# A squared-ReLU MLP by seven block products: the down stage run product by product, sums of its weights kept in DRAM, the up results stored without splitting

## The chip, the cores and the metric

The kernel runs on 1 core of one Trainium2 chip. A core has a matrix engine (TensorE, PE in the rows), a vector engine (DVE), a scalar engine (ACT), GpSimd (POOL) and a sync engine (SP), which run their own instruction streams in order and wait for each other by semaphores. PE writes its sums into eight PSUM banks; all other data lies in SBUF tiles of 128 partitions or in DRAM, and moves between the two by DMA. The metric is the device time of one execution in microseconds (us); lower is better.

## The reference, cut to what matters

```python
def sq_relu_mlp(h, w1, w2):
    return jnp.square(jax.nn.relu(h @ w1)) @ w2
...
        x = x_mid + gt_f * sq_relu_mlp(modulate(rms_norm(x_mid, g_ffn[l]), sh_f, sc_f),
                                       w_ff1[l], w_ff2[l])
    return rms_norm(x, g_final)
```

h is 1024 x 1024, w1 1024 x 4096, w2 4096 x 1024, all in 32-bit floats. Ahead of this stand a modulated norm, an input projection, retention heads, latent attention and the output projection; they make x_mid and are not touched.

## The kernel before

**Numbers.** A product of two 32-bit matrices is made from three matmuls: each operand is split into a rounded half (hi, type fp32r, written by ACT with a cast) and the rest (lo, a subtraction on DVE); hi·hi, hi·lo and lo·hi are summed in PSUM (`split`, lines 102 to 104, `mm3`, lines 97 to 100).

**Seven products.** Both matrix products of the MLP are done on 2 x 2 blocks with seven block products (numbered q = 1 to 7) instead of eight. Their operands are blocks or sums of blocks, and the seven results are added into the four result blocks: products 1, 6 and 7 one after the other into one PSUM sum ("a"), 5 and 3 into another ("c"), 2 and 4 into one each.

**Up stage.** Loop over 16 pairs p of 128 + 128 hidden columns. For each (p, q), `prep1` splits a piece of w1 (casts at L103, subtractions at L104), `mm_1` issues 12 matmuls of 128x512, and `post1` empties the bank: the copy at L1177 takes the sum of (p,6) out before (p,7) may add to the same bank, L1179 does so after (p,7), L1162 after (p,2). Relu and square are L1143 and L1144. With the last product, (p,3), the four hidden blocks c11, c12, c21, c22 are there; four subtractions and additions on DVE make the operands s1 to s4 of the down stage. c11 is stored in DRAM as `uda`, c21 and c22 as `udy`, s1 and s2 as `udz`, s3 and s4 as `udw`. `store_u` splits y, z and w before storing (cast L1152, subtraction through the helper at L94) and stores both halves (L1154, L1155), 1 MB for each instead of 512 KB.

**Down stage.** The contraction is cut into NB = 4 blocks b of GB = 4 pairs. The outer loop runs over b, the inner over the products q = 2, 1, 6, 5, 3, 7, 4. A step (b, q) has 4 row tiles k of 12 matmuls; after each, the bank is added to the result tiles `acc` in SBUF (a copy at L1271 the first time). `load_u` fetches the stored halves over POOL's DMA queue (L1237; `uda` over SP), `load_w2` the four blocks of w2 over SP (L1211), `chain_w2` and `chain2_w2` make the sums T1 to T4 of w2 blocks with `pairop` (L1085), and `prep2` splits the w2 operand. For the last block w2 is multiplied by the gate beforehand (`gate_w2`). The residual x_mid (`xm`) is added by `to_mid` along the way, and `final` normalizes and writes a row tile.

**Order.** All work is issued from Python loops in program order; a scheduler then orders each engine's stream by its own estimates. SBUF comes from a pool of 45 slots of 512 KB (`sl.get`, `sl.put`): a freed slot goes to the end of a queue and the next request takes the first. An instruction that gets a slot waits for the last user of it, which may be a DMA that still stores from it. In the up stage, `order` is the list of the (p, q), and `prep1` runs LEAD + 1 = 5 entries ahead; e = -1 is its last entry. In the last 11 entries the first loads and splits of the down stage are mixed in.

Of the kernel before, what the change touches and what calls it, by code (L numbers as in the profile page):

```python
# [12 lines left out]
F32 = mybir.dt.float32  # L13
# [40 lines left out]
def hymba_block(ctx: ExitStack, tc: tile.TileContext, A, K, out):  # L54
# [987 lines left out]
    while pend:  # L1042
# [115 lines left out]
    def post1(p, q):  # L1158
# [13 lines left out]
        if q == 1:  # L1172
            tt(c11, ps, c11, ALU.add)
            sqrelu(c11)
            store_u("a", p, x_, x_[0][:, 0:1])
        elif q == 6:
            S.copy(out=c12, in_=ps)  # L1177
        elif q == 7:
            S.copy(out=c21, in_=ps)  # L1179
            unbank(p, q)  # L1180
            tt(c22, bank(p, 5), c21, ALU.add)
        elif q == 4:
            tt(c21, c21, ps, ALU.subtract)
            unbank(p, q)
            sqrelu(c21)
            sqrelu(c22)
        elif q == 3:
            tt(c12, ps, c12, ALU.add)
            unbank(p, q)
            sqrelu(c12)  # L1190
            z, w = sl.get((2, 512)), sl.get((2, 512))
            s1, s2, s3, s4 = z[0][:, 0], z[0][:, 1], w[0][:, 0], w[0][:, 1]
            tt(s1, c12, c22, ALU.add)
            tt(s2, s1, c11, ALU.subtract)
            tt(s3, c11, c12, ALU.subtract)
            tt(s4, c21, s2, ALU.subtract)
            store_u("y", p, y_, y_[0])
            store_u("z", p, z, z[0])
            store_u("w", p, w, w[0])
            sl.put(x_)  # L1200
            cq.pop(p)

    w2r, w2v = {}, w_ff2.rearrange("(g i p) c -> i p g c", i=2, p=P)

    def load_w2(b, qs=("B21", "B11", "B12", "B22")):
        for q in qs:
            i, j = BH[q]
            w2r[b, q] = [sl.get((2, 512)) for _ in range(GB // 2)]
            for v, r in enumerate(w2r[b, q]):
                g = b * GB + 2 * v  # L1210
                nc.sync.dma_start(out=r[0], in_=w2v[i, :, g:g + 2, j * 512:(j + 1) * 512])  # L1211

    def chain_w2(b):
        n = GB // 2
        r = lambda q: w2r[b, q]
        for q in ("T1", "T2"):
            w2r[b, q] = [sl.get((2, 512)) for _ in range(n)]
        pairop(V, r("T1"), r("B12"), r("B11"), ALU.subtract)
        pairop(V, r("T2"), r("B22"), r("T1"), ALU.subtract)
        pairop(V, r("B12"), r("B22"), r("B12"), ALU.subtract)  # L1220
        w2r[b, "T3"] = w2r.pop((b, "B12"))

    def chain2_w2(b):
        pairop(V, w2r[b, "B21"], w2r[b, "B21"], w2r[b, "T2"], ALU.subtract)
        w2r[b, "T4"] = w2r.pop((b, "B21"))
        sl.put(*w2r.pop((b, "T2")))

    UOF = {1: ("a", 0), 2: ("y", 0), 4: ("y", 1), 5: ("z", 0), 6: ("z", 1), 7: ("w", 0), 3: ("w", 1)}
    ur, ab = {}, {}

    def load_u(b, q):
        n, k = UOF[q]
        vs = (0,) if n == "a" else (0, 1)
        ur[b, q] = [[sl.get((2, 512), F32 if n == "a" else F32R) for _ in range(GB // 2)] for _ in vs]
        for x_ in vs:
            for v, r in enumerate(ur[b, q][x_]):
                (nc.sync if n == "a" else nc.gpsimd).dma_start(out=r[0], in_=ud[n, b, x_][:, k, 2 * v:2 * v + 2, :])  # L1237

    def prep2(b, q):
        u_, w_ = ur.pop((b, q)), w2r[b, BOF[q]]  # L1240
        new = lambda: [[sl.get((2, 512), F32R) for _ in range(GB // 2)] for _ in range(2)]
        if len(u_) == 1:
            raw, u_ = u_[0], new()
            for v in range(GB // 2):
                split(raw[v][0], u_[0][v][0], u_[1][v][0])
            sl.put(*raw)
        ab[b, q] = [u_, new()]
        for v in range(GB // 2):
            split(w_[v][0], ab[b, q][1][0][v][0], ab[b, q][1][1][v][0])
        if q not in (2, 6):  # L1250
# [4 lines left out]
    def mm_2(b, q, k):
        (ah, al), (bh, bl) = ab[b, q]
        key = (b, k, {1: "a", 6: "a", 7: "a", 2: "b", 5: "c", 3: "c", 4: "d"}[q])
        if key not in pb:
            pb[key] = pF()
        ps = pb[key]  # L1260
        w = slice(k * P, (k + 1) * P)
        for g in range(GB):
            v, i = g // 2, g % 2
            mm3(ps, ah[v][0][:, i, w], al[v][0][:, i, w], bh[v][0][:, i], bl[v][0][:, i],
                q in (1, 2, 4, 5) and g == 0, g == GB - 1, q in (3, 6, 7))
        lo_, hi_ = slice(0, 512), slice(512, 1024)
        t0, t1 = acc[k][0], acc[4 + k][0]
        for o, first in {1: [(t0[:, lo_], False)], 2: [(t0[:, lo_], True)], 6: [(t0[:, hi_], True)], 5: [(t1[:, hi_], True)],
                         3: [(t0[:, hi_], False)], 7: [(t1[:, lo_], True), (t1[:, hi_], False)], 4: [(t1[:, lo_], False)]}[q]:
            if first and b == 0:  # L1270
                S.copy(out=o, in_=ps)  # L1271
            else:
                tt(o, ps, o, ALU.add)
# [7 lines left out]
    def load_xm(t):  # L1281
        xr_[t] = sl.get((1024,))
        nc.sync.dma_start(out=xr_[t][0], in_=xm[t])

    fs = {}

    def final(t):
# [3 lines left out]
        n = 2 if t == NT - 1 else 1  # L1291
# [77 lines left out]
    steps2 = [(b, q) for b in range(NB) for q in (2, 1, 6, 5, 3, 7, 4)]  # L1369
    for s, (p, q) in enumerate(order):  # L1370
# [3 lines left out]
        print("S", s - len(order), s, p, q, len(sl.free), file=open("/tmp/sl.txt", "a"))  # L1374
# [31 lines left out]
    for t in range(NT):
        acc[t] = sl.get((1024,))
    HALF = slice(0, 512), slice(512, 1024)

    def gate_w2(b, q, v):  # L1410
        r = w2r[b, q][v]
        tt(r[0], r[0], bc[5][0][:, HALF[BH[q][1]]].unsqueeze(1).broadcast_to([P, 2, 512]), ALU.mult)

    def load_xm(t, h):
        xr_[t, h] = tmp()
        nc.sync.dma_start(out=xr_[t, h], in_=xm[t][:, HALF[h]])

    def to_mid(t, h):
        w = acc[t][0][:, HALF[h]]
        tt(w, w, bc[5][0][:, HALF[h]], ALU.mult)  # L1420
        tt(w, w, xr_.pop((t, h)), ALU.add)

    s0 = 7 * (NB - 2)
    mids = [[(k, 0) for k in range(4)], [(k, 1) for k in range(4)], [(4 + k, 1) for k in range(4)], [(4 + k, 0) for k in range(4)]]
    side = {}
    for g, a in zip(mids, (s0 + 2, s0 + 6, s0 + 8, s0 + 10)):
        for n, m in enumerate(g):
            side.setdefault((a + n // 2, 1 + n % 2 * 2), []).append(lambda m=m: to_mid(*m))
            side.setdefault((a + n // 2 - 1, n % 2 * 2), []).append(lambda m=m: load_xm(*m))
    for n, (q, v) in enumerate([(q, v) for q in ("B21", "B11", "B12", "B22") for v in range(GB // 2)]):  # L1430
        side.setdefault((s0 + 4 + n // 4, n % 4), []).append(lambda q=q, v=v: gate_w2(NB - 1, q, v))

    def squares(t, h):
        if t not in fs:
            fs[t] = small.tile([P, 2], F32, name=f"fs{t}", tag=f"fs{t}", bufs=1)
        S.activation(out=tmp(), in_=acc[t][0][:, HALF[h]], func=AF.Square, accum_out=fs[t][:, h:h + 1])

    for s, (b, q) in enumerate(steps2):
        last = b == NB - 1
# [70 lines left out]
```

## Time and profile before

| | |
|---|---|
| median of 3 runs | 1331.37 us (1330.32 to 1335.32) |
| profiled execution | 1329.17 us, span 1327.4 us |
| PE busy | 1275.3 us, 96% of the span, 6665 matmuls |
| DVE busy | 973.9 us (73%) |
| ACT busy | 644.5 us (49%) |
| SP's DMA queue (q1) | 156.56 MB |
| POOL's DMA queue (q0) | 58.49 MB |
| mean granted PE clock | 0.988 of full |

The up stage's products with stores run from about 692 us, the down stage from about 1000 us to 1318 us. The tail behind it is the last normalization and its store. "Busy" for PE is modelled: a matmul is shown 0.39 us long although the next starts 0.227 us later, so idle time stands out only in the rows on waits and in counts of matmuls per stretch.

### The profile page before, as it was taken

To read this page: it belongs to the slowest core of one execution; us is meant where nothing else is said; L and a number is where in the kernel's file an instruction comes from. 1 tells how busy PE (TensorE), PEld (TensorE's weight loads), DVE (VectorE), ACT (ScalarE), POOL (GpSimd) and SP (SyncE) were. 2 spreads that over 40 slices of the span, in tenths; PEclk is the share of its full clock that TensorE was granted. 3 is DMA by queue.
4 is the path that set the end of the run, shared out by engine and by line. 5 is a ranking of instruction groups with operands and counts; after the bars stand their busy time and mean duration, and the time that the engine had idled before them with its cause. 6 is when DMAs were issued, how large, how long until landed. Compare 5 with 4: busy or idle time off the path is not lost.

```text
span 1327.4 us, 18159 instructions
## 1 busy us (share of the span) xinstructions
PE 1275.3 (96%) x6665; PEld 1086.9 (82%) x6665; DVE 973.9 (73%) x1950; ACT 644.5 (49%) x1349; POOL 73.4 (6%) x133
## 2 busy tenths in 40 slices
PE   7899999999999999999999799999987999999997
PEld 7788888999999898878788578887866788887885
DVE  5898576664777767984796788878767374876976
ACT  1851256754556545732475576766654231221233
POOL 0100000000000000000000000000001111111110
PEclk9999999999999999999999899999989999999999
DMA  9508401300001004362521577765799958577753
GB/s 348 213 3 290 153 28 53 100 13 0 1 9 36 9 25 143 104 214 96 162 84 51 211 276 247 270 225 205 245 338 341 373 159 289 202 257 259 215 158 125
DMA packets 98667, 216.73 MB, mean 163 GB/s; under 512 B 9353, under 2 KB 29522, under 8 KB 98578
## 3 DMA queue, kind: packets, MB, share of 16 engines
q1 hardware_dynamic: 81634, 156.56, 34.0%
q0 software_dynamic: 16368, 58.49, 13.3%
q8 instruction: 52, 0.85, 0.3%
q10 hardware_dynamic: 576, 0.53, 0.1%
q14 instruction: 37, 0.30, 0.1%
HBM read 148.70 MB, written 66.85 MB: 162 GB/s over the span
## 4 chain that ended last, share of the span: by engine, by line
PE 51%; issue 30%; DMA 8%; DVE 6%; ACT 4%; POOL 1%; SPq 0%; DVEq 0%; ACTq 0%; POOLq 0%
PE ps L100 15%; PE ps L98 15%; PE ps L99 15%; DMA u<-in_w_ff_dram 3%; DVE u L94 2%; PE ps L280 2%; DMA udw<-u 1%; DVE u L104 1%; ACT u L1152 1%; PE ps L238 1%; DMA udy<-u 1%; DMA u<-udy 1%; ACT u L103 1%; DVE u L502 1%; DMA u<-k_tri_dram 1%
## 5 line engine op out<-in xcount | busy, mean ns | idle before, releaser
L98 PE MATMUL ps<-u,u 128*128 128x512 f32 (+3 forms) x1664 | 621.5, 375 | 27.8 <-ACT u L103 8.0
L100 PE MATMUL ps<-u,u 128*128 128x512 f32 (+3 forms) x1664 | 613.3, 370 | 2.6 <-DVE u L94 1.7
L99 PE MATMUL ps<-u,u 128*128 128x512 f32 (+3 forms) x1664 | 614.8, 370 | 0.0
L98 PEld LDWEIGHTS ps<-u,u 128*128 128x128 f32 x1664 | 315.4, 190 | 86.0 <-ACT u L103 10.4
L100 PEld LDWEIGHTS ps<-u,u 128*128 128x128 f32 x1664 | 314.7, 189 | 54.8 <-DVE u L104 2.3
L99 PEld LDWEIGHTS ps<-u,u 128*128 128x128 f32 x1664 | 315.3, 189 | 49.0 <-issue 0.5
L103 ACT CAST u<-u 128x1024 fp32r<-128x1024 f32 (+3 forms) x199 | 168.1, 862 | 228.5 <-PE ps L99 66.5
L94 DVE TENSOR_TENSOR u<-ps,u 128x512 f32<-128x512 f32 (+3 forms) x318 | 201.7, 648 | 87.0 <-PE ps L100 62.0
L104 DVE TENSOR_TENSOR u<-u,u 128x1024 fp32r<-128x1024 f32 (+4 forms) x197 | 189.2, 982 | 59.6 <-ACT u L103 50.1
L94 DVE TENSOR_TENSOR u<-u,u 128x512 f32<-128x512 f32 (+2 forms) x128 | 114.9, 919 | 35.2 <-DMA u<-in_w_ff_dram 15.1
L863 DVE TENSOR_REDUCE mx<-ps 128x1 f32<-128x512 f32 (+1 forms) x96 | 55.0, 594 | 25.8 <-PE ps L862 25.7
L1152 ACT CAST u<-u 128x1024 fp32r<-128x1024 f32 x48 | 49.3, 1049 | 35.6 <-DVE u L94 29.8
L897 ACT CAST u<-ps 128x512 fp32r<-128x512 f32 (+1 forms) x96 | 45.1, 530 | 21.2 <-PE ps L895 21.2
L1085 DVE TENSOR_TENSOR u<-u,u 128x1024 f32<-128x1024 f32 x40 | 47.7, 1216 | 3.4 <-DMA u<-in_w_ff_dram 3.3
L1143 ACT ACTIVATE u<-u 128x512 f32<-128x512 f32 x64 | 40.1, 627 | 20.2 <-DVE u L94 19.9
L874 ACT ACTIVATE u<-ps,nm 128x512 f32<-128x512 f32 x64 | 43.6, 691 | 11.8 <-DVE nm L867 11.8
L1144 ACT ACTIVATE u<-u 128x512 f32<-128x512 f32 x64 | 40.3, 631 | 1.1
L427 DVE SCALAR_TENSOR_TENSOR u<-u,sc,u 128x1024 f32<-128x1024 f32 x28 | 35.8, 1279 | 4.5 <-DMA u<-in_w_ada_dram 4.2
L1237 POOL DMA_DIRECT2D u<-udy x32 | 16.9, 534 | 371.7 <-DVE u L104 314.9
L858 PE MATMUL ps<-u,u 128*128 128x512 f32 (+1 forms) x96 | 37.1, 387 | 0.4 <-ACT u L837 0.2
L280 PE MATMUL ps<-u,u 128*128 128x128 f32 x224 | 29.1, 295 | 8.6 <-DMA u<-in_w_ada_dram 8.6
L104 DVE TENSOR_TENSOR u<-tmp,u 128x512 fp32r<-128x512 f32 x32 | 21.8, 687 | 19.3 <-ACT u L103 19.3
(209 smaller groups left out, 1290.1 us busy)
## 6 DMA issues: line engine op xcount, KB each, us to landing
u<-in_w_ff_dram SPq DMA_DIRECT2D x64, 512.0 KB, 7.0
u<-in_w_ada_dram SPq DMA_DIRECT2D x48, 512.0 KB, 5.5
udy<-u SPq DMA_DIRECT2D x32, 512.0 KB, 3.6
udz<-u SPq DMA_DIRECT2D x32, 512.0 KB, 3.8
udw<-u SPq DMA_DIRECT2D x32, 512.0 KB, 5.3
u<-udy POOLq DMA_DIRECT2D x32, 512.0 KB, 7.0
u<-udz POOLq DMA_DIRECT2D x32, 512.0 KB, 6.6
u<-udw POOLq DMA_DIRECT2D x32, 512.0 KB, 7.7
```

What stands on the lines that cost most here:

```text
L94: V.tensor_tensor(out=o, in0=a, in1=b, op=op)
L98: T.matmul(ps, lhsT=lh, rhs=rh, start=start, stop=False, **kw)
L99: T.matmul(ps, lhsT=lh, rhs=rl, start=False, stop=False, **kw)
L100: T.matmul(ps, lhsT=ll, rhs=rh, start=False, stop=stop, **kw)
L103: S.copy(out=hi, in_=raw)
L104: (eng or V).tensor_tensor(out=lo, in0=raw, in1=f(hi), op=ALU.subtract)
L280: T.matmul(mps[g][j // 4][:, j % 4, :], lhsT=w[:, j * P:(j + 1) * P], rhs=rhs, start=first and j % 4 == 0, stop=last and j % 4 == 3)
L863: V.reduce_max(out=mx[:, kb:kb + 1], in_=ps[:, 0:n], axis=AX.X)
L874: S.activation(out=dst[kb], in_=ps[:, 0:n], func=AF.Exp, scale=SCALE, bias=nm, accum_out=su[:, kb:kb + 1])
L897: S.copy(out=hi, in_=ps[:, 0:m, :])
L1085: eng.tensor_tensor(out=o[v][0], in0=a[v][0], in1=b[v][0], op=op)
L1152: S.copy(out=h[0], in_=ap)
```

## The change

- `store_u` stores y, z and w as they are: its casts, subtractions and second DMAs are gone. Each slot goes back to the pool after the stores. The splitting is done in the down stage, in `prep2`.
- GB becomes 2, so the contraction has NB = 8 blocks, and the outer loop of the down stage is the product: steps (q, b) for q = 2, 1, 6, 7, 4, 5, 3, each with all eight b. A PSUM bank keeps its sum over the eight steps; it is emptied after the last b alone (`evac2`). A step has 4 row tiles of 6 matmuls. In the last four steps of product 3 the row tile is the outer loop.
- A step loads its u operand (512 KB) and one or two w2 tiles (512 KB each), all over SP's queue. Product 1's steps make T1 = B12 - B11 and store it in DRAM (`td`), product 6's make T2 = B22 - T1 likewise; later steps load them back. Loads are issued up to six steps ahead, splits up to three.
- The gate is no longer folded into w2: `to_mid` multiplies result halves by it, and `evac2` does for product 3.

```diff
-    NP, GB = FF // 256, 4
+    NP, GB = FF // 256, 2
...
-    def store_u(q, p, r, ap):
-        if q == "a":
-            nc.sync.dma_start(out=ud[q, p // GB, 0][:, :, p % GB, :], in_=ap)
-            return
-        h = sl.get((2, 512), F32R)
-        lo = ap.bitcast(F32R)
-        S.copy(out=h[0], in_=ap)
-        tt(lo, ap, f(h[0]), ALU.subtract)
-        nc.sync.dma_start(out=ud[q, p // GB, 0][:, :, p % GB, :], in_=f(h[0]))
-        nc.sync.dma_start(out=ud[q, p // GB, 1][:, :, p % GB, :], in_=f(lo))
-        sl.put(h, r)
+    def store_u(q, p, ap):
+        nc.sync.dma_start(out=ud[q, p // GB][:, :, p % GB, :], in_=ap)
...
+    WOF = {2: ("B21",), 1: ("B11", "B12"), 6: ("B22", "T1"), 7: ("B22", "B12"), 4: ("B21", "T2"), 5: ("T1",), 3: ("B22",)}
+    steps2 = [(q, b) for q in (2, 1, 6, 7, 4, 5, 3) for b in range(NB)]
...
+    def load2(s):
+        q, b = steps2[s]
         n, k = UOF[q]
...
+        raw2[s] = r = [sl.get((2, 512)) for _ in range(1 + len(WOF[q]))]
+        nc.sync.dma_start(out=r[0][0], in_=ud[n, b][:, k])
+        for w, t in zip(WOF[q], r[1:]):
+            if w in BH:
+                i, j = BH[w]
+                nc.sync.dma_start(out=t[0], in_=w2v[i, :, b * GB:(b + 1) * GB, j * 512:(j + 1) * 512])
+            else:
+                nc.sync.dma_start(out=t[0], in_=td[w, b])
+
+    def prep2(s):
+        q, b = steps2[s]
+        u, w, *x_ = raw2.pop(s)
+        ab[s] = [sl.get((2, 512), F32R) for _ in range(4)]
+        split(u[0], ab[s][0][0], ab[s][1][0])
+        sl.put(u)
+        if q in (6, 7, 4):
+            tt(w[0], w[0], x_[0][0], ALU.subtract)
+        split(w[0], ab[s][2][0], ab[s][3][0])
+        if q == 1:
+            tt(x_[0][0], x_[0][0], w[0], ALU.subtract)
+            nc.sync.dma_start(out=td["T1", b], in_=x_[0][0])
         if q == 6:
...
+            nc.sync.dma_start(out=td["T2", b], in_=w[0])
+        sl.put(*x_, w)
...
+        else:
+            m = tmp()
+            tt(m, ps, bc[5][0][:, hi_], ALU.mult)
+            tt(t0[:, hi_], m, t0[:, hi_], ALU.add)
+            squares(k, 1)
+            final(k)
...
+        e = s - len(order)
+        if e in (-10, -8, -6, -4):
+            load2((10 + e) // 2)
+        if e in (-5, -3):
+            prep2((5 + e) // 2)
...
+        while nload < min(s + 7, len(steps2)):
+            load2(nload)
+            nload += 1
+        while nprep < min(s + 4, len(steps2)):
+            prep2(nprep)
+            nprep += 1
```

**Where ACT's stream moves.** The first place is ACT around the stores of pairs 0 and 1, while PE does (2,7), (3,7), (2,4), (3,4). In the kernel before, L1152 is `store_u`'s cast, and u512 is the w1 operand of (3,4), u520 and u518 those of (4,1) and (4,2):

```order
L1177 COPY u469_7606<-ps449_7701 128x512
L1152 CAST u509_7980<-u491_7809 128x1024
L1143 ACTIVATE u459_7542<-u459_7542 128x512
L1144 ACTIVATE u459_7542<-u459_7542 128x512
L1143 ACTIVATE u465_7570<-u465_7570 128x512
L1144 ACTIVATE u465_7570<-u465_7570 128x512
L1152 CAST u510_7985<-u507_7974 128x1024
L103 CAST u526_8116<-tmp_8117 128x512
L1152 CAST u511_7990<-u508_7975 128x1024
L103 CAST u528_8136<-tmp_8117 128x512
L103 CAST u512_7995<-u455_7517 128x512
```

In the changed kernel u509 is the operand of (3,4), u514 and u512 those of (4,1) and (4,2), and L1168 and L1170 are the copies that were L1177 and L1179:

```order
L1168 COPY u469_7626<-ps449_7721 128x512
L103 CAST u509_8003<-u455_7537 128x512
L1143 ACTIVATE u459_7562<-u459_7562 128x512
L1144 ACTIVATE u459_7562<-u459_7562 128x512
L103 CAST u514_8048<-u502_7938 128x512
L1143 ACTIVATE u465_7590<-u465_7590 128x512
L1144 ACTIVATE u465_7590<-u465_7590 128x512
L103 CAST u512_8030<-u503_7939 128x512
L1170 COPY u515_8063<-ps449_7721 128x512
```

The operand of (3,4) moves from behind three `store_u` casts to the place right behind the copy.

The second place is ACT at the end of the up stage, around the copy that lets PE go from (15,6) to (15,7), ps503. In the kernel before, the L103 cast of u743 is a split of a w2 tile and the two L1152 casts are `store_u` of pair 14:

```order
L1143 ACTIVATE u693_9745<-u693_9745 128x512
L1144 ACTIVATE u693_9745<-u693_9745 128x512
L103 CAST u743_10076<-u725_9980 128x1024
L1152 CAST u719_9962<-u716_9951 128x1024
L1152 CAST u720_9967<-u717_9952 128x1024
L1177 COPY u713_9910<-ps503_9916 128x512
```

In the changed kernel the casts of u700 and u698 are splits for steps 3 and 2 of the down stage (the u operand of (2,3) and the w2 tile of (2,2)):

```order
L1143 ACTIVATE u654_9609<-u654_9609 128x512
L1144 ACTIVATE u654_9609<-u654_9609 128x512
L103 CAST u700_9938<-u681_9849 128x1024
L103 CAST u698_9932<-u675_9809 128x1024
L1168 COPY u667_9754<-ps503_9764 128x512
```

Three casts stood ahead of the copy, now two do; the two write into slots that (15,6) itself reads until it ends.

## Rows read from the trace of the kernel before

**Rows 1.** Windows, PE alone: start:end, length, busy (matmuls), clock, DMA share, GB/s

```profile
core 0: us, PE busy (x), PEclk, DMA share, GB/s
692.00:1317.80 625.80, 599.54 (x2590) 0.98 0.69 234
720.00:757.00 37.00, 29.18 (x107) 0.86 0.55 201
800.00:900.00 100.00, 100.00 (x441) 1.00 0.71 245
980.00:1000.00 20.00, 14.25 (x56) 0.83 0.94 324
1020.00:1050.00 30.00, 21.63 (x86) 0.89 1.03 359
1200.00:1240.00 40.00, 38.20 (x163) 1.00 0.69 234
```

**Rows 2.** Waits of PE from 692 to 1317.8 us: total, times, longest

```profile
PE ps L98 <- ACT u L103: 8.0, 3, 3.8
PE ps L98 <- ACT u L1177: 7.5, 3, 5.7
PE ps L98 <- DMA u<-udz: 7.5, 1, 7.5
```

**Rows 3.** Timeline of ACT, 733 to 752 us: start, duration, ..., [idle before <-releaser]

```profile
738.89 1.04 ACT L1152 CAST u<-u 128x1024 fp32r<-128x1024 f32 x1 [3.29 <-DMA udy<-u]
...
749.68 0.62 ACT L103 CAST u<-u 128x512 fp32r<-128x512 f32 x1 [2.73 <-DMA udz<-u]
```

**Rows 4.** Timeline of ACT, 983 to 993 us

```profile
988.34 1.04 ACT L103 CAST u<-u 128x1024 fp32r<-128x1024 f32 x1 [3.28 <-DMA u<-in_w_ff_dram]
989.29 1.99 ACT L1152 CAST u<-u 128x1024 fp32r<-128x1024 f32 x2
991.19 0.58 ACT L1177 COPY u<-ps 128x512 f32<-128x512 f32 x1
```

**Rows 5.** Timeline of PE, the two longest waits of the later stages

```profile
991.82 0.80 PE L98 MATMUL ps<-u,u 128*128 128x512 f32 x1 [5.75 <-ACT u L1177]
...
1028.60 2.90 PE L98 MATMUL ps<-u,u 128*128 128x512 f32 x6 [7.48 <-DMA u<-udz]
```

**Rows 6.** Groups by form, 692 to 990 us: count, busy, mean ns, idle before

```profile
L1152 ACT CAST u<-u 128x1024 fp32r<-128x1024 f32 x44 | 45.2, 1049 | 29.1 <-DVE u L94 23.3 <-DMA udy<-u 3.3 <-PE ps L100 2.1
```

**Rows 7.** Groups by form, 1040 to 1310 us

```profile
L104 DVE TENSOR_TENSOR u<-u,u 128x1024 fp32r<-128x1024 f32 x52 | 62.2, 1218 | 20.4 <-ACT u L103 16.6 <-PE ps L99 3.3
L103 ACT CAST u<-u 128x1024 fp32r<-128x1024 f32 x52 | 54.0, 1054 | 151.4 <-PE ps L99 65.0 <-PE ps L100 59.1 <-DVE u L104 27.0
```

**Rows 8.** Windows with SP alone: length, SP busy, PE clock, DMA share, GB/s

```profile
0.00:40.00 40.00, 0.96 0.96 356
960.00:1000.00 40.00, 0.91 0.93 322
1000.00:1060.00 60.00, 0.94 1.04 365
```

**Rows 9.** Timeline of SP, 975 to 1010 us

```profile
978.19 1.35 SPq L1211 DMA_DIRECT2D u<-in_w_ff_dram  x2
...
1008.08 0.52 SPq L1154 DMA_DIRECT2D udz<-u  x1
```

**Rows 10.** DMA issues by tile: times, size, median us to landing

```profile
udy<-u SPq DMA_DIRECT2D x32, 512.0 KB, 3.6
...
u<-udy POOLq DMA_DIRECT2D x32, 512.0 KB, 7.0
```

**Rows 11.** Timeline of the tail, DVE's first and last of these chains

```profile
1310.06 0.69 DVE L94 TENSOR_TENSOR u<-ps,u 128x512 f32<-128x512 f32 x1 [1.43 <-PE ps L100]
...
1312.97 0.16 DVE L94 TENSOR_TENSOR xr<-xy,xq 128x1 f32<-128x1 f32 x1
...
1318.39 0.68 DVE L94 TENSOR_TENSOR u<-ps,u 128x512 f32<-128x512 f32 x1
...
1322.38 0.16 DVE L94 TENSOR_TENSOR xr<-xy,xq 128x1 f32<-128x1 f32 x1
```

More of the change, by code (lines that the diff above doesn't have):

```diff
@@ L1174, in post1 @@
             sqrelu(c11)
-            store_u("a", p, x_, x_[0][:, 0:1])
+            store_u("a", p, x_[0][:, 0:1])
         elif q == 6:
@@ L1190, in post1 @@
             sqrelu(c12)
+            store_u("y", p, y_[0])
             z, w = sl.get((2, 512)), sl.get((2, 512))
@@ L1194, in post1 @@
             tt(s2, s1, c11, ALU.subtract)
+            store_u("z", p, z[0])
             tt(s3, c11, c12, ALU.subtract)
             tt(s4, c21, s2, ALU.subtract)
[L1197 to L1200, printed above, removed]
+            store_u("w", p, w[0])
+            sl.put(x_, y_, z, w)
             cq.pop(p)
[L1203 to L1226, printed above, removed]
@@ L1255, in mm_2 @@
[L1255 to L1260, printed above, removed]
-        w = slice(k * P, (k + 1) * P)
[L1262 to L1273, printed above, removed]
+    w2v = w_ff2.rearrange("(g i p) c -> i p g c", i=2, p=P)
@@ new lines, in hymba_block, with mm_2 @@
+    pk = {}
+    def mm_2(s, k, gs=range(2)):
+        q, b = steps2[s]
+        if b == 0 and q in (2, 1, 4, 5) and gs[0] == 0:
+            psn[0] += 1
+            i = fbank.popleft()
+            fbank.append(i)
+            pk[GRP[q], k] = psp.tile([P, 512], F32, name=f"ps{psn[0]}", tag=f"b{i}", bufs=1)
+        ps = pk[GRP[q], k]
+        ah, al, bh, bl = (t[0] for t in ab[s])
+        w = slice(k * P, (k + 1) * P)
+        for i in gs:
+            mm3(ps, ah[:, i, w], al[:, i, w], bh[:, i], bl[:, i], q in (1, 2, 4, 5) and b == 0 and i == 0,
+                b == NB - 1 and i == 1, q in (3, 6, 7))
@@ L1406, in hymba_block @@
[L1406 to L1439, printed above, removed]
-        if s + 2 < len(steps2):
-            load_u(*steps2[s + 2])
-        if s + 1 < len(steps2):
-            if s > 0:
-                prep2(*steps2[s + 1])
-            if steps2[s + 1][1] == 2:
-                chain_w2(b + 1)
-        if b == NB - 2 and q == 2:
+        e = s - len(order)
@@ L1448, in hymba_block @@
             load_bc5()
-        if q == 5 and b + 1 < NB:
-            load_w2(b + 1)
-        if last and q == 6:
+        if q == 4 and b == 0:
             gfin = sl.get((1024,))
             nc.sync.dma_start(out=gfin[0], in_=A["g_final"].partition_broadcast(P))
-        for k in range(4):
-            mm_2(b, q, k)
-            for fn in side.get((s, k), ()):
-                fn()
-            if last and q == 3:
-                squares(k, 0)
-                squares(k, 1)
-                final(k)
-            if last and q == 7:
-                squares(4 + k, 1)
-            if last and q == 4:
-                squares(4 + k, 0)
-                final(4 + k)
@@ L1467, in hymba_block @@
-        for x_ in ab.pop((b, q)):
-            for h_ in x_:
-                sl.put(*h_)
+        if b == NB - 1 and q in (2, 7):
+            for k in range(4):
+                acc[k + 4 * (q == 7)] = sl.get((1024,))
+        if s < tail:
+            for k in range(4):
+                mm_2(s, k)
+                if b == NB - 1:
+                    evac2(q, k)
+            sl.put(*ab[s])
+        elif s == len(steps2) - 1:
+            for k in range(4):
+                for x_ in range(tail, len(steps2)):
+                    mm_2(x_, k)
+                evac2(q, k)
@@ new lines, in hymba_block @@
+        for _ in range(2):
+            if side:
+                side.popleft()()
+        if b == NB - 1 and q in (1, 6, 4, 5):
+            t0, h = {1: (0, 0), 6: (0, 1), 4: (4, 0), 5: (4, 1)}[q]
+            ms = [(t0 + k, h) for k in range(4)]
+            side.append(lambda m=ms[0]: load_xm(*m))
+            for m, nx in zip(ms, ms[1:] + [None]):
+                if nx:
+                    side.append(lambda m=nx: load_xm(*m))
+                side.append(lambda m=m, q=q: to_mid(*m, q != 6))
+                if q == 5:
+                    side.append(lambda m=m: final(m[0]))
```

86 lines of the change are left out of this document (42 added, 44 removed).

## The prediction

> **What bounds the kernel now.** I read the page's first line first: PE is busy 96% of the span, and nothing else is above 73%. A busy PE is not a dense one, so next come windows of PE alone with its counts. From 800 to 900 us 441 matmuls start in 100 us at clock 1.00: one per 0.2268 us, the pitch of an unhindered PE [rows 1]. From 692 us, where the stores begin, to 1317.8 us, the end of the last product, there are 2590 matmuls in 625.8 us; at 0.2268 us they need 587.4 us. The excess, 38.4 us, is all that this change can win on PE, and I look for its places. 720 to 757 us holds 107 matmuls, 24.3 us of work, so 12.7 us are lost; 980 to 1000 us loses 20 - 56 x 0.2268 = 7.3; 1020 to 1050 us loses 30 - 86 x 0.2268 = 10.5; 1200 to 1240 us loses 3.0 [rows 1]. Some 4.9 us are scattered. In the first three the granted clock is 0.86, 0.83 and 0.89 of full: a part of each ran at 1.2 GHz instead of 2.4 after PE had waited.
>
> Then the waits of PE: three for an L103 cast (8.0 us), three for the L1177 copy (7.5), one for a load of `udz` (7.5) [rows 2]. Followed back on the timelines:
> - 720 to 757 us: ACT stands in `store_u`'s cast (L1152) for 3.29 us, until a `udy` store has left the slot it writes to, and in a prep cast for 2.73 us, until a `udz` store has left [rows 3]. The casts that PE needs are queued behind.
> - 980 to 1000 us: ACT waits 3.28 us for a w2 tile, then does two L1152 casts (1.99 us), then the copy that PE stood still for, 5.75 us in all [rows 4, 5].
> - 1020 to 1050 us: block 0's `udz` halves come back late, after 7.48 us [rows 5].
>
> **The change, part by part.**
>
> *The casts and subtractions of `store_u` leave the up stage.* Of the cast there are 48, 44 of them after 692 us, at 1049 ns [rows 6]: 3 per pair, 3.1 us of ACT and as many subtractions of DVE in 19.1 us of PE work per pair (7 products x 12 matmuls x 0.2268). This work was beside PE's, so it costs nothing by itself. What counts is that it stood ahead of L1177 and the prep casts. Half of the stored bytes go too (3 x 512 KB per pair), and a store landed in 3.6 us [rows 10], so the slots come back earlier. In the changed order (3,4)'s operand stands right behind the copy. I take 12.7 + 4.9 of the excess as gone, less what stays: (4,7)'s copy still has a cast ahead that takes a slot from a `udz` store, about 0.5 (0 to 1), and thinner cover at the products' ends, about 0.5 (0 to 2).
>
> *The splits move to the down stage.* A step there is 24 matmuls, 5.44 us of PE. It needs two casts (2 x 1.054 = 2.1 us of ACT) and two subtractions and, in four products, a difference of w2 tiles (3 x 1.218 = 3.7 us of DVE) [rows 7]. Both are under 5.44 and issued three steps ahead: I take 0 for them. The low bound is 0, since the work was hidden before; the high one is what DVE does beside it in the steps of one product that empty banks, 4 more operations in the last step of 8, at 0.7 each [rows 11]: 3.7 + 2.8 = 6.5, 1.1 over for one step, which the three steps of lead cover.
>
> *Product by product.* Matmuls are as many (1344). Product 2 uses only B21 and y, for eight steps (43.5 us); `udz` is wanted from product 5 on. So the 7.48 us wait for block 0's `udz` and the half clock behind it have no cause: -10.5. Block boundaries end too: -3.0. A boundary between products needs a bank only once every 8 steps; 0 (bound 3.0, the loss from 1200 to 1240 us [rows 1]).
>
> *The copy at (15,7).* In the changed order two casts still stand ahead of it, splits for steps 3 and 2, into slots that (15,6)'s matmuls read to their end. So they start when (15,6) ends: 2 x 1.0 + 0.58 for the copy [rows 4, 7] = 2.6 us after it, against five matmuls of another bank that PE still has ahead of (15,7), 1.1 us. I take a wait of 1.4 us; so of this stretch's 7.3 us there stay 1.4. Bounds: 0, and all of the 7.3 as before.
>
> *DMA in the down stage.* 18 tiles x 8 blocks x 0.524 MB = 75.5 MB of loads, 8.4 MB of `td` stores, 4.2 of x_mid, 4.2 of output: 92.3 MB, over 304.8 us (1344 x 0.2268) 303 GB/s, all on SP's queue. The densest are the 16 steps of products 1 and 6, with three loads and a store, 2.10 MB in 5.44 us: 385 GB/s. The rows show 356 GB/s at a DMA share of 0.96, 365 at 1.04, 322 at 0.93 [rows 8]. At 365 a step takes 5.75 us, 5 us late after 16; at 322 6.5 us, 17 us late. Slots let loads run 8 steps ahead, 43.5 us, so this lead covers both; I take 0. Issuing costs SP 0.52 to 0.68 us a DMA [rows 9], 2.3 us a step. A `td` store also stands ahead of later loads in SP's stream and waits for DVE's subtraction; it is that of four steps before, so done.
> A DMA of 512 KB alone landed in 3.6 us [rows 10], and on its way among others moved at 365 GB/s, 1.44 us each [rows 8]; so DMAs overlap. The Trainium skill, DMA: Bandwidth & Descriptors (Anatomy of one DMA; Bandwidth), speaks against this: it fits one DMA at about 2.0 us plus bytes at 436 GB/s, and asks for 1 MiB or more per DMA to reach 75% of peak. By that, taken one after the other, 512 KB cost an estimated 3.2 us and a heavy step 12.8 us; 16 of them end some 75 us later than PE could with its lead, and the kernel would come out near 1370 us. The lone landing time agrees with the page, the rate in the stretch does not, so I go by the stretch.
>
> *Tail.* The last row tiles end one whole 5.44 us (24 matmuls) apart instead of 2.72. Before, from the last evacuation to the chain's last small operation took 1318.39 to 1322.38 + 0.16 = 4.15 us, while an unhindered one took 1310.06 to 1312.97 + 0.16 = 3.07: -1.1. The gate costs one more DVE operation, +0.69 [rows 11]. Sum -0.4.
>
> **Sum.** -38.4 + 1.4 + 0.5 + 0.5 - 0.4 = -36.4. The profiled execution took 1329.17 us, so 1292.8; the median of the runs lies 2.2 above it: 1295 us. Its own range is 1288 (all bounds low, and -2 for the spread of runs) to 1300.
>
> **Rivals.**
> 1. *The end of up keeps its wait.* For: the casts ahead of the copy are long, and a wait of 1.4 may bring the half clock as 5.75 did. Against: no DMA is waited for. All 7.3 instead of 1.4: +5.9, 1301 us. 0.13.
> 2. *The early waits were not the casts'.* ACT still takes slots in turn, and [rows 3]'s second wait is of a prep cast, not of `store_u`. For: the pool hands out slots in the same turn as before. Against: fewer bytes, fewer slots in stores. 12.7 and some 2 of the scattered stay: 1310 us. 0.08.
> 3. *The waits go, the clock does not.* If low clock had another cause than the waits, only the waits go. Of 38.4 then 23.0 [rows 2] and some 3 scattered: 12 stay, 1307 us. The change would not do what the rows promise. Against: 1.00 wherever PE does not wait. 0.04.
> 4. *SP's queue becomes the bound* (the other side). The mean over 692 to 1317.8 us is 234 GB/s, and 234 again at 1200 to 1240 [rows 1]; there nothing asked for more, but if slots, stores and loads on one queue hold it at that, 92.3 MB take 394 us. They have 304.8, plus 27 us (loads begin 10 up products before its end), plus the 36.4 gained: 368 us, 251 GB/s. Above some 258 GB/s nothing shows; near 251 the gain is eaten; at 234 it is +26, 1358 us. 0.10, half of it near 251 (no change), half below.
>
> **How the numbers follow.** My forecast has 0.65, the rivals 0.13, 0.08, 0.04 and 0.10. 0.5% of the median, 6.7 us, is about what a measurement here tells from nothing. Forecast and rivals 1 to 3 are faster by more: 0.90. Rival 4 gives 0.05 same, 0.05 slower. The range 1288 to 1313 takes in rivals 1 to 3 with their own spread and leaves out rival 4 and a part of the edges.
>
> **What would show it.** Right: no PE wait above 1.5 us after 720 us; 441 matmuls per 100 us at clock 1.00 through the down stage; one wait at (15,7), for the copy L1168, near 1.4 us; DMA at 350 GB/s or so in product 1 and 6 without a PE wait for a load of `ud`, `td` or w2; a last chain of about 3.8 us behind PE. Wrong: waits of casts on DMA stores in the first pairs (rival 2), low clock without a wait (rival 3), PE waiting for casts or loads from product 1 on, with SP's queue full (rival 4).

## The result and the profile after

The changed kernel takes 1292.87 us (median of 4 runs, 1290.95 to 1293.94), the kernel before 1330.84 us beside it: a ratio of 0.9712, 95% interval 0.9679 to 0.9744. The forecast was 1295 us. The profiled execution took 1293.10 us (span 1291.3), 36.07 us less than before's; the sum said 36.4.

PE alone by windows, in the columns of [rows 1] (start:end, length, busy, matmuls, clock, DMA share, GB/s):

```profile
692.00:1282.30 590.30, 589.87 (x2599) 1.00 0.64 228
720.00:757.00 37.00, 37.00 (x165) 1.00 0.52 180
800.00:900.00 100.00, 100.00 (x441) 1.00 0.45 150
980.00:1000.00 20.00, 20.00 (x89) 1.00 0.99 328
1020.00:1050.00 30.00, 30.00 (x134) 1.00 1.04 413
1200.00:1240.00 40.00, 40.00 (x178) 1.00 0.58 203
```

2599 matmuls in 590.3 us are 0.2271 us each, the pitch of the undisturbed stretch, at clock 1.00. (A window counts a matmul that it cuts, so a short one shows one or two too many.) What PE waits for from 692 us on, beside the 23.0 us of [rows 2]:

```profile
PE ps L98 <- DVE u L94: 0.4, 1, 0.4
```

To see where the 36 us went, count matmuls: both kernels issue 6665, and the start of the n-th can be compared (0.2 us at the first of them).

| matmuls | place | lost (+) or won (-) from before to after, us | foreseen |
|---|---|---|---|
| to 4000 | ahead of the up stage's stores | +2.0 | 0 |
| 4200 to 4300 | first pairs, 720 to 757 us | -12.5 | -12.7 |
| 4300 to 5200 | three small places | -3.2 | -4.9 + 0.5 + 0.5 |
| 5200 to 5300 | end of the up stage | -7.6 | -7.3 + 1.4 |
| 5400 to 5500 | block 0's `udz` | -10.9 | -10.5 |
| 6100 to 6300 | block boundary | -3.3 | -3.0 |
| behind PE | tail | -0.5 | -0.4 |

ACT still stands for stores, twice in the stretch that answers to [rows 3] (timeline, idle before and its releaser in brackets), but now PE has its operands in time:

```profile
735.96 0.62 ACT L103 CAST u<-u 128x512 fp32r<-128x512 f32 x1 [1.30 <-DMA udz<-u]
...
758.26 0.62 ACT L103 CAST u<-u 128x512 fp32r<-128x512 f32 x1 [1.38 <-DMA udz<-u]
```

The end of the up stage, which answers to [rows 4, 5]. First ACT:

```profile
967.37 2.01 ACT L103 CAST u<-u 128x1024 fp32r<-128x1024 f32 x2 [1.03 <-PE ps L99]
969.28 0.57 ACT L1168 COPY u<-ps 128x512 f32<-128x512 f32 x1
```

Then PE at that place; the row at 968.53 is the last of (15,6), five matmuls of another product follow, and 969.90 is the first of (15,7):

```profile
968.53 0.39 PE L100 MATMUL ps<-u,u 128*128 128x512 f32 x1
...
969.66 0.39 PE L99 MATMUL ps<-u,u 128*128 128x512 f32 x1
969.90 0.50 PE L98 MATMUL ps<-u,u 128*128 128x512 f32 x1
```

The wait that I had put at 1.4 us is about 0.1. The two casts ahead of the copy do wait for (15,6), but not for its end: its h operand fills separate slots for its two halves (`bh[k // 2]`, `bl[k // 2]` in `mm_1`), and the first half is read for the last time by the fifth and sixth of the twelve matmuls. The first cast starts at 967.37, just after the sixth has begun, and the second before the twelfth (968.53).

DMA from 1000 to 1060 us, in the heavy steps (a summary line, then size and median us from issue to landing):

```profile
DMA packets 8960, 24.62 MB, mean 410 GB/s; under 512 B 750, under 2 KB 750, under 8 KB 8955
...
u<-in_w_ff_dram SPq DMA_DIRECT2D x16, 512.0 KB, 10.1
```

And the last evacuation and the last small operation of the tail, as in [rows 11]:

```profile
1282.63 0.69 DVE L94 TENSOR_TENSOR tmp<-ps,u 128x512 f32<-128x512 f32 x1 [0.33 <-PE ps L100]
...
1286.27 0.16 DVE L94 TENSOR_TENSOR xr<-xy,xq 128x1 f32<-128x1 f32 x1
```

That is 1286.27 + 0.16 - 1282.63 = 3.80 us, against 4.15 before.

### The profile page after: what moved, and what is told of

It reads as the page before. It is cut to its first block, busy times and chain, and to the rows that moved or that the text cites. A ratio compares the mean times of both kernels' runs of the same rounds, so it can differ in the third digit from the quotient of the medians.

```text
span 1291.3 us, 18056 instructions
## 1 busy us (share of the span) xinstructions
PE 1266.7 (98%) x6665; PEld 1084.7 (84%) x6665; DVE 908.8 (70%) x1850; ACT 647.5 (50%) x1349; POOL 22.6 (2%) x37
## 4 chain that ended last, share of the span: by engine, by line
PE 61%; issue 31%; DVE 3%; DMA 2%; ACT 2%; POOL 1%; DVEq 0%; ACTq 0%; POOLq 0%
PE ps L100 19%; PE ps L98 19%; PE ps L99 19%; PE ps L280 2%; DVE u L104 1%; PE ps L238 1%; DVE u L94 1%; DVE u L502 1%; DMA u<-k_tri_dram 1%; PE ps L496 1%; DMA u<-in_w_ada_dram 0%; ACT u L103 0%; PE ps L587 0%; POOL y_dram L933 0%; PE ps L580 0%
## 5 line engine op out<-in xcount | busy, mean ns | idle before, releaser
L98 PEld LDWEIGHTS ps<-u,u 128*128 128x128 f32 x1664 | 313.6, 188 | 55.9 <-DVE u L94 3.5
L100 PEld LDWEIGHTS ps<-u,u 128*128 128x128 f32 x1664 | 313.5, 188 | 53.0 <-DVE u L94 2.1
L99 PEld LDWEIGHTS ps<-u,u 128*128 128x128 f32 x1664 | 313.8, 189 | 48.5 <-issue 0.5
L104 DVE TENSOR_TENSOR u<-u,u 128x1024 fp32r<-128x1024 f32 (+4 forms) x245 | 248.1, 1030 | 107.4 <-ACT u L103 99.5
L103 ACT CAST u<-u 128x1024 fp32r<-128x1024 f32 (+3 forms) x247 | 217.6, 900 | 198.0 <-DVE u L94 58.4
L94 DVE TENSOR_TENSOR u<-ps,u 128x512 fp32r<-128x512 f32 (+3 forms) x218 | 134.4, 632 | 68.4 <-PE ps L100 52.3
L94 DVE TENSOR_TENSOR u<-u,u 128x512 f32<-128x512 f32 (+1 forms) x104 | 88.0, 850 | 38.7 <-ACT u L1144 18.0
L103 ACT CAST u<-tmp 128x512 fp32r<-128x512 f32 x32 | 19.8, 620 | 36.6 <-DVE u L94 27.2
L858 PE MATMUL ps<-u,u 128*128 128x512 f32 (+1 forms) x96 | 37.1, 387 | 0.3 <-ACT u L837 0.2
L280 PEld LDWEIGHTS ps<-u,u 128*128 128x128 f32 x224 | 29.7, 218 | 8.8 <-issue 5.2
L895 PE MATMUL ps<-ident,u 128*128 128x128 f32 x256 | 35.1, 274 | 0.3 <-DVE nm L867 0.2
L861 PE MATMUL ps<-u,u 128*128 128x512 f32 (+1 forms) x96 | 34.5, 359 | 0.0
```

The costliest lines, as they stand in the source:

```text
L94: V.tensor_tensor(out=o, in0=a, in1=b, op=op)
L98: T.matmul(ps, lhsT=lh, rhs=rh, start=start, stop=False, **kw)
L99: T.matmul(ps, lhsT=lh, rhs=rl, start=False, stop=False, **kw)
L100: T.matmul(ps, lhsT=ll, rhs=rh, start=False, stop=stop, **kw)
L103: S.copy(out=hi, in_=raw)
L104: (eng or V).tensor_tensor(out=lo, in0=raw, in1=f(hi), op=ALU.subtract)
```

## The experiments

The change has three separable parts: single instead of double stores of y, z, w; single instead of double loads of them; the order product by product. The theory was that the first removes the early waits and the third the wait for `udz`. "Double" stores come with `store_u`'s cast and subtraction; with single loads the down stage does the split instead. Each kernel was timed beside the kernel before on its chip; the table has the ratio to it with its 95% interval.

| order | stores | loads | median us | ratio |
|---|---|---|---|---|
| block by block (before) | double | double | 1331 to 1334 | 1 |
| block by block | double | single | 1327.24 | 0.9960 (0.9946 to 0.9974) |
| block by block | single | double | 1304.87 | 0.9787 (0.9760 to 0.9813) |
| block by block | single | single | 1298.02 | 0.9737 (0.9719 to 0.9755) |
| by product | double | double | 1353.63 | 1.0163 (1.0098 to 1.0228) |
| by product | double | single | 1310.98 | 0.9852 (0.9826 to 0.9879) |
| by product (changed) | single | single | 1292.87 | 0.9712 (0.9679 to 0.9744) |

**The split put back into `store_u`.**

```diff
     def store_u(q, p, ap, r=None):
...
+        h = sl.get((2, 512), F32R)
+        lo = ap.bitcast(F32R)
+        S.copy(out=h[0], in_=ap)
+        tt(lo, ap, f(h[0]), ALU.subtract)
+        nc.sync.dma_start(out=ud[q, p // GB][:, :, p % GB, :], in_=f(h[0]))
+        nc.sync.dma_start(out=ux[q, p // GB][:, :, p % GB, :], in_=f(lo))
+        sl.put(h, r)
```

> The changed kernel with the split put back into store_u (cast, subtraction, both halves stored, in the old places); the down stage is the new one and reads the stored high halves (the low halves are stored and not read). Theory A (the casts of store_u, waiting for slots that stores still hold, stand ahead of the casts that PE needs): the first pairs lose their 12.5 us again, the scattered places 2 to 3.5 us, the end of up up to 7.6 us: 1306 to 1317 us, with PE waiting for L103 casts between 735 and 760 us. Rival B (the early waits belong to the turn of the slots, that is to the rest of the kernel, not to these casts): within 3 us of 1293 us. Later than the up stage both expect nothing.

1310.98 us: theory A; B falls. Between the 4200th and 4300th matmul this kernel loses 12.1 us against the changed one, between the 4400th and 4500th 1.6, and at the end of the up stage (5200th to 5300th) 1.0, nothing like 7.6. But it also loses 3.6 us between the 5700th and 6000th, in the down stage, where neither theory expected any; its loads of u are issued 23 to 32 us ahead of steps 8 to 23 there, against 38 to 45 in the changed kernel, but whether that is the reason is open. Its window of PE in the first pairs, and ACT in it (the cast is L1154 here, `ux` the second store):

```profile
720.00:757.00 37.00, 30.21 (x111) 0.86 0.55 199
```

```profile
738.25 1.04 ACT L1154 CAST u<-u 128x1024 fp32r<-128x1024 f32 x1 [3.16 <-DMA uxy<-u]
...
749.12 0.62 ACT L103 CAST u<-u 128x512 fp32r<-128x512 f32 x1 [2.80 <-DMA udz<-u]
```

These are the two rows of [rows 3] again, 0.6 us earlier and of nearly the same length.

**Its two halves apart: the work without the stores, the stores without the work.**

```diff
+            h = sl.get((2, 512), F32R)
+            S.copy(out=h[0], in_=ap)
+            tt(h[0], ap, f(h[0]), ALU.subtract)
+            sl.put(h)
```

> The changed kernel; store_u stores unsplit, and does the cast and the subtraction besides into a slot that it gives back at once, with nothing of it stored. It has ACT's and DVE's added work and one more slot request per store, not the added bytes. Theory A in its sharp form (the price is the wait for a store that holds a slot): stores are 16 x 1.57 MB fewer and slots come back sooner, so a part stays, +3 us (0 to 8). Rival C (ACT's 3.1 us of casts per pair are the price): as much as the full split, +12 us or more. Rival D (the bytes are the price): 0.

```diff
+            nc.sync.dma_start(out=ux[q, p // GB][:, :, p % GB, :], in_=ap)
```

> The changed kernel with each store of y, z and w done twice (the second to a tensor that nobody reads): the added bytes and the longer hold of the slots, no cast and no subtraction. Theory A: prep casts alone can meet held slots, so 0 to +4 us. Rival D (the bytes are the price): +12 us in the first pairs and some more at the end of up. Rival C: 0.

1296.30 us (ratio 0.9730, 0.9715 to 0.9745) and 1295.19 us (0.9718, 0.9703 to 0.9734): neither differs from the changed kernel beyond its interval (in the profile of the first some 3 us are lost, spread from the 4400th to the 5400th matmul). The first pairs' window of each, the casts first:

```profile
720.00:757.00 37.00, 37.00 (x164) 1.00 0.46 160
```

```profile
720.00:757.00 37.00, 37.00 (x165) 1.00 0.75 261
```

With 261 GB/s the second moves more than the kernel before did there (201), and PE is dense. So neither ACT's 3.1 us per pair nor the bytes are the price; C and D fall. The two together cost 12 us; by the rows of the run before, what costs is a cast that must take a slot which a double store still holds. (With the split the stores are also issued later, behind cast and subtraction; no run parts this from the hold of the slots.)

**The unsplit stores alone, in the old order.** `store_u` and `post1` as in the changed kernel, the rest as before, with

```diff
-        vs = (0,) if n == "a" else (0, 1)
...
+        ur[b, q] = [[sl.get((2, 512)) for _ in range(GB // 2)]]
+        for v, r in enumerate(ur[b, q][0]):
+            (nc.sync if n == "a" else nc.gpsimd).dma_start(out=r[0], in_=ud[n, b][:, k, 2 * v:2 * v + 2, :])
```

> The kernel before with the unsplit stores alone: its down stage (four blocks of four pairs, seven products inside a block, loads of u over POOL) fetches u whole and splits it there. Theory A: the 12.5 us of the first pairs and the scattered 3.4 us are won, of the 7.6 us at the end of up some part; the 10.9 us of block 0's udz and the 3.3 us at a block boundary stay: 1331 - 16 to 24 = 1307 to 1315 us. Rival E (the late udz was a matter of doubled bytes and slots, not of the order of products): the 10.9 us go too, 1297 to 1303 us. Rival B: no better than 1325 us.

1298.02 us: nearly the whole gain, and the range of rival E, not of my theory. PE's windows (first pairs; end of up; the stretch in which before waited for `udz`, here earlier; part of the later blocks):

```profile
720.00:757.00 37.00, 37.00 (x165) 1.00 0.52 174
960.00:980.00 20.00, 17.62 (x71) 0.91 0.85 287
1000.00:1030.00 30.00, 30.00 (x134) 1.00 0.74 260
1160.00:1200.00 40.00, 40.00 (x178) 1.00 0.55 198
```

The 10.9 us and the 3.3 us are gone without any change of order. What stays is one wait at the end of up, where a cast waits for a load and the copy stands behind it:

```profile
971.15 2.51 ACT L103 CAST u<-u 128x1024 fp32r<-128x1024 f32 x3 [2.01 <-DMA u<-uda]
973.57 0.57 ACT L1167 COPY u<-ps 128x512 f32<-128x512 f32 x1
```

It costs 3.5 us against the changed kernel (a wait of PE of 2.4 and the lower clock behind it).

**Stores or loads?** First the kernel before with loads of one half alone; then the kernel of unsplit stores alone, with every y, z and w tile loaded twice. The second leaves out the splitting of y, z and w altogether, in both stages; its edit is shown against that kernel.

```diff
-        vs = (0,) if n == "a" else (0, 1)
+        vs = (0,)
```

> The kernel before with its split stores as they were, but the down stage (old order) loads the high halves alone, one tile instead of two, and splits them again; the low halves are stored and not read. Theory L (the late udz at the start of the down stage comes of the doubled loads, which fill the queue and hold slots): the 12.5 us of the first pairs and the scattered 3 us stay, the 10.9 us of block 0 and the 3.3 us at the boundary go: 1331 - 14 = 1317 us (1311 to 1320). Theory S (it comes of the doubled stores of the last pairs and their subtractions, which stand behind w2 sums on DVE): the 10.9 us stay, 1325 to 1331 us.

```diff
-        for v, r in enumerate(ur[b, q][0]):
...
+        for x_ in vs:
+            for v, r in enumerate(ur[b, q][x_]):
+                (nc.sync if n == "a" else nc.gpsimd).dma_start(out=r[0], in_=ud[n, b][:, k, 2 * v:2 * v + 2, :])
```

> The kernel before with unsplit stores, and each y, z and w tile loaded twice over POOL's queue into the two tiles that held the halves; they are used as they come, so the split of y, z and w is left out everywhere (the second tile is not the rest of the first). Old order, doubled loads, single stores. Theory L: the first pairs' 12.5 us are won, the 10.9 us of block 0 stay: 1309 to 1316 us. Theory S: both are won, 1297 to 1302 us.

1327.24 and 1304.87 us. With double stores and single loads PE still loses 6.9 us at the start of the down stage (5400th to 5500th matmul; 10.9 before), and 3.4 more just ahead of it; with single stores and double loads it loses nothing at either place. So in the old order this loss goes with the stores, as theory S said, and L falls. The windows of PE from 1000 to 1050 us, stores double first, then loads double:

```profile
1000.00:1050.00 50.00, 42.63 (x174) 0.93 0.84 288
```

```profile
1000.00:1050.00 50.00, 50.00 (x223) 1.00 0.80 277
...
1150.00:1230.00 80.00, 76.54 (x333) 1.00 0.75 244
```

The block boundary is the loads' (76.54 of 80 us busy, 4.9 us lost; with single loads its 3.3 us are gone with either kind of store). How double stores make `udz` late shows on DVE in the kernel before: a sum of w2 tiles waits for a load, the last pair's s4 (1018.36) and its subtractions (1020.10) stand behind it, and behind these the evacuations of product 1 (1024.64):

```profile
1013.81 4.63 DVE L1085 TENSOR_TENSOR u<-u,u 128x1024 f32<-128x1024 f32 x4 [2.47 <-DMA u<-in_w_ff_dram]
1018.36 0.68 DVE L94 TENSOR_TENSOR u<-u,u 128x512 f32<-128x512 f32 x1
...
1020.10 3.49 DVE L94 TENSOR_TENSOR u<-u,u 128x1024 fp32r<-128x1024 f32 x3
...
1024.64 1.28 DVE L94 TENSOR_TENSOR u<-ps,u 128x512 f32<-128x512 f32 x2
```

POOL's load of `udz` then takes a slot that this chain frees:

```profile
1021.82 0.53 POOL L1237 DMA_DIRECT2D u<-udz  x1 [9.92 <-DVE u L94]
```

But a late `udz` is not all of it. With double stores and single loads no wait of PE for `udz` is left. PE waits at that place all the same, 4.17 us for an evacuation on DVE, which stands behind the same subtractions of `store_u`:

```profile
1024.08 3.49 DVE L94 TENSOR_TENSOR u<-u,u 128x1024 fp32r<-128x1024 f32 x3
...
1029.33 0.68 DVE L94 TENSOR_TENSOR u<-ps,u 128x512 f32<-128x512 f32 x1
```

```profile
1030.16 0.47 PE L98 MATMUL ps<-u,u 128*128 128x512 f32 x1 [4.17 <-DVE u L94]
```

The two timed kernels show that in the old order the stores decide; that these chains are how, I read from the rows and did not test alone.

**The new order alone**, with double stores and both halves loaded over POOL and used unsplit:

```diff
+        v = 1 if n == "a" else 2
...
+        (nc.sync if v == 1 else nc.gpsimd).dma_start(out=r[0][0], in_=ud[n, b][:, k])
+        if v == 2:
+            nc.gpsimd.dma_start(out=r[1][0], in_=ul[n, b][:, k])
```

> The new down stage (product by product, weight sums in DRAM) with the old up stage: halves stored by store_u, both halves of y, z and w fetched over POOL as before, not split again. Theory: the first pairs lose 12.5 us as before, the scattered places 3, the end of up up to 7.6. In the down stage the loads grow by one tile in six of seven products: product 6's eight steps ask for 2.62 MB in 5.44 us, 482 GB/s; at the 410 GB/s that the changed kernel's trace shows there, 8 steps fall 8 us behind of a lead of some 40, so nothing is lost: 1306 to 1317 us. Rival (DMA's rate binds, the unsplit loads are what makes the order possible): the down stage loses 10 us or more besides, over 1320 us, with PE waiting for loads from product 6 on.

1353.63 us, slower than before: the rival. Of the 60.4 us by which PE ends later than in the changed kernel, 27.7 are lost between the 5600th and the 6000th matmul. PE's windows there, one dense and two not, all with the queues full:

```profile
1040.00:1060.00 20.00, 20.00 (x90) 1.00 1.05 403
...
1100.00:1120.00 20.00, 10.56 (x30) 0.66 1.05 412
...
1160.00:1180.00 20.00, 14.97 (x50) 0.74 1.07 395
```

At the longest wait PE starts product 6 in the bank that product 1's evacuation must leave, and DVE has that evacuation behind a difference of w2 tiles that waits for `td`:

```profile
1103.42 1.22 DVE L94 TENSOR_TENSOR u<-u,u 128x1024 f32<-128x1024 f32 x1 [4.88 <-DMA u<-tdT]
...
1107.85 0.68 DVE L94 TENSOR_TENSOR u<-ps,u 128x512 f32<-128x512 f32 x1
```

```profile
1108.58 0.79 PE L98 MATMUL ps<-u,u 128*128 128x512 f32 x1 [7.94 <-DVE u L94]
```

What the parts do together shows in the losses against the changed kernel's profile, at two places: the end of up (5200th to 5400th matmul) and the start of down, where before waited for `udz` (5400th to 5500th):

| stores, loads | end of up, by block | by product | start of down, by block | by product |
|---|---|---|---|---|
| double, double | 7.6 | 17.2 | 10.9 | 0.0 |
| double, single | 11.7 | 0.5 | 6.9 | 0.0 |
| single, double | 4.2 | not run | 0.0 | not run |
| single, single | 3.6 | 0 | 0.1 | 0 |

The loss at the start of down goes in either of two ways: with single stores in the old order, or with the order by product, in each pairing run. At the end of up the parts do not add up. Of the 17.2 us, 9.5 are lost at a copy that waits for a slot from the store of a low half (`ul`):

```profile
1008.08 0.58 ACT L1181 COPY u<-ps 128x512 f32<-128x512 f32 x1 [7.06 <-DMA ulz<-u]
```

So with double stores the order is worth a ratio of 0.9960 to 0.9852 when loads are single, and costs time when they are double.

**Is the queue at its limit?** Copies from DRAM to DRAM were no test:

```diff
+        if q in (1, 6):
+            for _ in range(n):
+                nc.sync.dma_start(out=dx.pop(), in_=w2v[0, :, b * GB:(b + 1) * GB, 0:512])
```

> The changed kernel with one more 512 KB copy from DRAM to DRAM on SP's queue in each of the 16 steps of products 1 and 6 (nobody reads it): 2.62 MB in 5.44 us, 482 GB/s asked. At 410 GB/s a step takes 6.4 us, 15 us behind after 16 steps, of a lead of 43.5 us. Theory (the lead of the loads covers a queue that is too slow for a while): no change, within 2 us of 1293. Rival (the queue is at its limit, the lead is not there): +10 to +15 us.

> The same with three more copies in each of these steps: 3.67 MB in 5.44 us, 675 GB/s asked. At 410 GB/s a step takes 8.95 us, 56 us behind after 16 steps; less the lead of 43.5 us: +12.7 us by the theory of the lead, more by a few us if PE drops to the lower clock in its waits; 1303 to 1315 us. With no lead it would be +56 us. If copies within DRAM move slower than 410 GB/s, more in both.

1295.18 and 1293.30 us, but they tell nothing of the down stage: the copies wait for nothing, and the scheduler issued them between 58 and 182 us of the span, long before that stage. Tied to data, as three more stores of the same tile behind each store of T1 and T2, they stay in place:

```diff
             nc.sync.dma_start(out=td["T1", b], in_=x_[0][0])
+            for _ in range(3):
+                nc.sync.dma_start(out=dx.pop(), in_=x_[0][0])
```

> The changed kernel with each store of T1 and T2 done four times (three go to tensors that nobody reads), behind the same subtraction: in the 16 steps of products 1 and 6 3.67 MB are asked for in 5.44 us, 675 GB/s. At the 410 GB/s of the queue a step takes 8.95 us: 56 us behind after 16 steps; with a lead of 43.5 us, +12.7 us, and a few more if PE drops to the lower clock. If the lead does not count, +56 us. If the queue has room beyond 410 GB/s, or stores go beside loads, less than +5 us.

1326.38 us (0.9954, 0.9934 to 0.9974), 33.5 us over the changed kernel. PE is dense to 1060 us, then waits, while the queue moves what it can:

```profile
1060.00:1080.00 20.00, 15.82 (x55) 0.83 1.03 416
...
1120.00:1140.00 20.00, 15.58 (x46) 0.74 1.04 415
```

So 405 to 417 GB/s is the ceiling here, and it costs only when the lead is used up. Pairing each load of u with the step that uses it, the issue is 38 to 45 us ahead in the changed kernel's steps 8 to 23; here it shrinks from 42 to 15. The last 15 us cannot be spent: a load lands in 10.1 us, and a split follows. Of the 56 us that the expectation reckoned the queue to fall behind, the usable lead pays 42 - 15 = 27. The remaining 29 compare with 31.9 us that PE loses between the 5600th and the 6000th matmul, 18.4 of them in waits and the rest at the lower clock. (The extra stores also hold their slots longer, which this run doesn't separate.)

**Does the lookahead in the code set the lead?** Loads three and two steps ahead instead of six, splits two and one instead of three:

```diff
-        while nload < min(s + 7, len(steps2)):
+        while nload < min(s + 3, len(steps2)):
...
-        while nprep < min(s + 4, len(steps2)):
+        while nprep < min(s + 2, len(steps2)):
```

> The changed kernel with loads issued up to three steps ahead instead of six, splits up to two instead of three. A load has 16 us from its issue to its step less 5.44 for the split; under full queues loads landed in 9.5 us. Theory of the lead: in the heavy 16 steps (385 GB/s asked, 410 given) nothing piles up, so three steps are just enough: 0 to +5 us. Rival (the six steps are what carries the heavy stretch): +10 us or more, with waits of PE for casts from product 1 on.

> The changed kernel with loads issued up to two steps ahead (six before) and splits one (three before). A load that lands in 9.5 us and a split that takes 3.7 us on DVE want 13.2 us; the loads have 10.9 us. So PE waits in the heavy steps, by up to 2.3 us each for 16 steps: +10 to +37 us, more with the lower clock. If the slots and the order of the queues set the real lead and not these numbers, within 3 us of 1293.

1294.26 (0.9718) and 1292.33 us (0.9692, 0.9667 to 0.9717): no difference. The arithmetic of the second expectation was wrong, since loads were still issued 24 us or more ahead of their steps in both. The shorter numbers do cut the lead (to 24 to 40 us in steps 8 to 23), but far less than they say; what sets the rest, the scheduler or the slots, these runs do not show.

No experiment points to a version that beats the changed kernel: from 692 us on PE has 0.4 us of waits left.

## Why the prediction was right, and where its reasons were not

- *What there was to win*: right. The excess over the undisturbed pitch, 38.4 us, was named, and 37.6 us of it went. Waits and the lower clock behind them went together, so rival 3 (the clock stays) falls: the granted clock is 1.00 in every window shown.
- *Casts and subtractions of `store_u`*: right in place and size (12.7 foreseen, 12.5 measured, 12.1 back when undone). The step gave two mechanisms, the queue of ACT and the hold of the slots; the runs show that it takes both. Rival 2 falls, though ACT's waits for stores that it spoke of remain.
- *"Product by product ... the 7.48 us wait for block 0's `udz` and the half clock behind it have no cause: -10.5. Block boundaries end too: -3.0"*: the time came, and the order does what the step says: by product no kernel loses anything at either place, not even with double stores and double loads. But it was not needed: both losses also go with the old order kept, the first with single stores, the second with single loads. So the weak point of the step is that it gave these 13.5 us to the order alone; the unsplit stores win them without it. The order by product, on top of both, moves the ratio from 0.9737 (0.9719 to 0.9755) to 0.9712 (0.9679 to 0.9744), which these runs don't tell from nothing; the profiles differ by 5.7 us, 3.5 of them in one wait at the end of up. I had read "waits for a load of `udz`" as a question of when `udz` is needed, and had not followed back why the load was issued late, which stood on POOL's and DVE's rows; nor had I seen that product 1's evacuations stood behind the same chain.
- *The copy at (15,7)*: 1.4 us foreseen, 0.1 measured, since the first half's slots come free after half of (15,6); rival 1 falls. From 692 us on the sum said -38.4 + 2.4 = -36.0 and -37.6 came; 2.0 us were lost ahead of the stage, where I had put 0. These two errors nearly cancel, which is luck.
- *Splits in the down stage, 0*: right; no wait of PE for an L103 or L104 appears there.
- *DMA, 0, and rival 4*: the forecast was right; the queue gave 410 GB/s for 385 asked, more than the 365 reckoned with. As a mechanism rival 4 is real: two kernels here lost 28 and 32 us behind full queues, by their profiles. But its threshold was wrong: by its own terms nothing would show above 92.3 MB in 304.8 + 27 us, 278 GB/s, not 258; and a mean rate of 251 GB/s over the stage says little: with the threefold extra stores the mean load is 92.3 + 48 x 0.524 = 117 MB in the same 368 us, 319 GB/s and far under the ceiling, and 33.5 us are lost, in the sixteen steps that ask for 675. The local rate against the ceiling, less the usable lead, is the measure.
 The Trainium skill, DMA: Bandwidth & Descriptors (Bandwidth), asks for 1 MiB or more per DMA to pass 75% of its 436 GB/s peak, and gives each core roughly 358 GB/s of DRAM when both cores of a pair stream. The trace does not agree with the first for a stream of overlapping DMAs: 512 KB each, 410 GB/s. One core runs here, so no run shows the second.
- *Tail*: -0.4 foreseen, -0.5 measured.

## What to carry to other kernels

A wait named after a DMA is only the last link: follow the load back to when it was issued, and to what its slot and the instruction ahead of it waited for, before giving a reordering alone the credit for its removal. On an engine that works in order, an instruction that waits for a transfer (a cast that takes a slot still being stored, a sum of tiles still being loaded) must not stand ahead of one that PE needs; in the first pairs, taking away either the instruction or the double store removed the wait. When a change has separable parts, time the corners: here unsplit stores with single loads gave 34 of 38 us in the old order, the new order alone made the kernel slower, and what the order was worth hung on the loads.

## What was not expected of the hardware

One wait far ahead of the change, some 2 us for DVE, is followed by the lower clock in ten of the fourteen profiles and not in the other four, with no clean relation to its length. Before and after (the first matmul behind the wait; then PE's window from 585 to 590 us):

```profile
583.89 0.50 PE L98 MATMUL ps<-u,u 128*128 128x512 f32 x1 [2.07 <-DVE u L94]
```

```profile
584.41 0.69 PE L98 MATMUL ps<-u,u 128*128 128x512 f32 x1 [2.24 <-DVE u L94]
```

```profile
585.00:590.00 5.00, 5.00 (x24) 1.00 0.65 232
```

```profile
585.00:590.00 5.00, 5.00 (x17) 0.70 0.68 239
```

With a wait of 1.82 us (T1 and T2 stored four times) the clock in that window was 0.70, with 2.49 us (high halves loaded alone) it was 1.00. Here it costs 1.8 us of the 2.0 that the changed kernel loses ahead of the stage.
